# Seven products for pairs of output tiles in the q, k, v projections of a two-layer backbone step

## The chip, the cores and the metric

The kernel runs on one core of a Trainium2 chip. The metric is the device time of one execution in microseconds (us). The text calls the engines by their profile names: PE is TensorE's matmuls and PEld its weight loads, DVE is VectorE, ACT is ScalarE, POOL is GpSimd, SP is SyncE, which here only issues DMAs.

## The reference

The step runs a trunk of two layers over 1152 tokens of width 1024: 128 prompt tokens and 1024 latent tokens. Layer 0 mixes tokens by a gated long convolution, layer 1 by differential attention over 8 heads with rotary positions for the latent tokens. Each layer is followed by a feed-forward with a depthwise convolution of width 3. Every part has a norm ahead of it and one behind it, with shift, scale and gate from a small matrix product of the condition (the modulation). Cut to what the change touches:

```python
hp = modulate(rmsnorm(xp, norm_w[i, 0]), mp[0], mp[1])
hs = modulate(rmsnorm(xs, norm_w[i, 0]), ms[0], ms[1])
qp, kp, vp = qkv_heads(hp, at_w_qkv[j])           # h @ w_qkv: 1024 -> 3 * 1024
qs, ks_, vs = qkv_heads(hs, at_w_qkv[j])
qs = rope_2d(qs, cos_s, sin_s)                    # x * cos + rot * sin
ks_ = rope_2d(ks_, cos_s, sin_s)
ys = diff_attention(qs, k_all, v_all, ...)        # scores scaled by 64 ** -0.5 = 0.125

def conv_ffn(h, w_up, w_dw, b_dw, w_down):
    u = dwconv3(h @ w_up, w_dw, b_dw)
    g, val = jnp.split(u, 2, axis=-1)
    return (jax.nn.silu(g) * val) @ w_down
```

## The kernel before

The 1152 tokens are nine tiles of 128, T0 (the prompt) to T8, in three chunks of three tiles. The code counts the chunks 0, 1 and 2; the change's title calls them 1, 2 and 3. Activations lie with the model's width on the partitions (8 pieces of 128, index `k`) and tokens in the free dimension. To keep float32 precision every operand is split into `hi` (rounded) and `lo` (the rest), and each product is made as hi·hi + hi·lo + lo·hi, three matmuls. `split` (L214) does it: ScalarE writes `hi` (L215), then VectorE subtracts (L220); with `dma=True` ScalarE also writes `-hi` (L217) and GpSimd issues a DMA that adds the source to it (L218).

The stages follow each other: layer 0's mixer, its feed-forward, the projections to q, k, v, the attention, layer 1's feed-forward. What each engine does stands in the order in which the code was recorded; each engine takes its own row of instructions strictly one after the other and waits on the others by semaphores. So the order of the calls in the Python code decides what can hide behind what. Side work is written as generators: `advance(queue, n)` takes `n` steps of the queued ones, `advance(queue, -1)` runs the queue out, and `next(extra)` takes one row of the modulation's weights (a 512 KB load `adaw` and two DVE passes, L379).

*Feed-forward.* Chunk 0 goes group by group (up, convolution, down). Chunks 1 and 2 of the up projection go together by seven products: the weights of an output pair are a 2x2 block matrix (output tile by half of the inner dimension), the two chunks' activations another, and seven products of blocks with sums of blocks take the place of eight. `combine` makes the seven operands of the activations (`pair`, with `t` for the differences, ACT L553 and DVE L547, L560); the table `ALONG` says in which of the seven slots of a step the loads, the sums of the weights (`total`), their splits (`high`, `low`, `both`) and the evacuations of the banks are issued, and how many steps ahead. Slots from -19 on run along the last groups of chunk 0 (`along2`). The down projection of chunk 1 and then of chunk 2 follows (`down`), three or two weight tiles a group.

*Projections* (`groups`). 24 output tiles of 128, in the order q0 k0 v0 q1 k1 v1 ... (`ORDER`). For each tile and chunk a group of 24 matmuls (L1646 to L1648: 8 pieces by 3 products) of 386 or 384 columns; the first three tiles go chunk by chunk, the next 18 tile by tile, the last three together. ACT takes a group out of its bank, for chunk 0 in two pieces (L1652 the prompt, L1653 two latent tiles), else in one (L1655), and scales q by 0.125. The split of tile i+1 (`split_w`) is issued right behind the first of tile i's three groups. While the first groups run, the pre-norms of T6 to T8 are finished (POOL L457 `xn`, PE transposes L470, ACT L473, DVE L480 and L481). When a tile's three groups are there, `finish` turns q and k by position: eight DMAs of POOL (L1565) swap rows into `rot`, three DVE operations (L951) multiply and add, the result is split and stored. PE also does the prompt's own attention there, head by head (`Context`).

## Time and profile before

| what | time |
|---|---|
| median of 3 runs | 3126.3 us (3124.62 to 3126.78) |
| the profiled execution | 3126.71 us |
| its span from first to last instruction | 3124.9 us |
| projections within it, 1524.9 to 1855.3 | 330.4 us |
| down groups of the first feed-forward, chunk 1, 1333 to 1425 | 92 us |

The profiled execution's own time is 1.8 us more than its span, which lies around the instructions. The trace names source lines with L; matmuls are pipelined, so that the durations of two neighbours overlap, and the distance of their starts is what one costs. Behind "<-" in brackets stands what ended a wait, and ahead of it how long the engine had been idle.

### The profile page before, as it was taken

The numbers are of one execution on the slowest core, as the hardware profiler recorded it, in microseconds if no ns is written. First come the engines' busy times: TensorE is split into PE (matmuls) and PEld (weight loads), VectorE is DVE, ScalarE is ACT, GpSimd is POOL, SyncE is SP. The second block draws the span as 40 slices with busy tenths as digits, with TensorE's granted clock in tenths as the row PEclk, the third lists the DMA queues.
The fourth block names the chain that finished last, engine by engine and source line by source line (L and its number), as shares of the span: only waits on it lengthen the run. The fifth ranks groups of instructions, "written<-read, shape, count | busy, mean of one in ns | idle before, by whom it ended". The sixth has DMA issues, their size and how long they took to land. (4 is left out here: it accounts for less than half of the span.)

```text
span 3124.9 us, 46695 instructions
## 1 busy us (share of the span) xinstructions
PE 3044.9 (97%) x17332; PEld 2823.7 (90%) x17332; DVE 2143.6 (69%) x3057; ACT 1729.7 (55%) x3185; POOL 619.2 (20%) x1010
## 2 busy tenths in 40 slices
PE   8999999999998999999999999999999999999998
PEld 5999999778888999988899999999888998999987
DVE  5778888756676787776563347789565756777743
ACT  5454445545544777655533348899545546777532
POOL 3111111220001222211143422223220002222100
PEclk9999999999999999999999999999999999999999
DMA  6455546754445898777464464353363246887763
GB/s 254 114 125 119 125 114 157 212 187 141 149 156 154 211 214 209 168 290 258 149 196 148 134 194 110 96 145 106 135 212 140 96 161 153 215 183 182 218 212 119
DMA packets 190136, 520.48 MB, mean 167 GB/s; under 512 B 25730, under 2 KB 53986, under 8 KB 189908
## 3 DMA queue, kind: packets, MB, share of 16 engines
q1 hardware_dynamic: 137428, 394.94, 37.9%
q0 software_dynamic: 52480, 122.56, 19.5%
q8 instruction: 136, 2.23, 0.3%
q14 instruction: 92, 0.75, 0.1%
HBM read 354.50 MB, written 68.13 MB: 135 GB/s over the span
## 5 line engine op out<-in xcount | busy, mean ns | idle before, releaser
L746 PE MATMUL banks<-pair,hi 128*128 128x386 f32 x2464 | 639.1, 341 | 10.0 <-DVE junk L599 9.8
L746 PEld LDWEIGHTS banks<-pair,hi 128*128 128x128 f32 x2464 | 453.2, 190 | 11.4 <-DVE junk L599 10.7
L215 ACT ACTIVATE hi<-wr 128x1024 fp32r<-128x1024 f32 (+1 forms) x400 | 365.2, 913 | 150.4 <-DMA wr<-ffn_up 47.6
L220 DVE TENSOR_TENSOR lo<-wr,hi 128x1024 fp32r<-128x1024 f32 x247 | 305.4, 1237 | 204.8 <-ACT hi L215 203.4
L746 PE MATMUL banks<-pair,lo 128*128 128x386 f32 x1232 | 419.1, 340 | 0.7 <-DMA lo<-wr 0.7
L218 POOL DMA_DIRECT2D lo<-wr x153 | 132.5, 866 | 860.9 <-ACT lo L217 637.4
L690 PE MATMUL banks<-lo,hi 128*128 128x512 f32 x792 | 250.2, 396 | 5.9 <-DVE lo L220 5.9
L690 PE MATMUL banks<-hi,hi 128*128 128x512 f32 x792 | 251.7, 398 | 2.3 <-ACT hi L215 2.3
L690 PE MATMUL banks<-hi,lo 128*128 128x512 f32 x792 | 249.9, 395 | 0.0
L667 PE MATMUL banks<-hi,hi 128*128 128x388 f32 x704 | 240.6, 342 | 8.5 <-ACT hc L510 8.2
L669 PE MATMUL banks<-hi,lo 128*128 128x388 f32 x704 | 239.1, 340 | 1.8 <-DVE lo L220 1.8
L668 PE MATMUL banks<-lo,hi 128*128 128x388 f32 x704 | 239.7, 340 | 0.0
L746 PEld LDWEIGHTS banks<-pair,lo 128*128 128x128 f32 x1232 | 233.3, 189 | 1.0 <-DMA lo<-wr 1.0
L1746 DVE TENSOR_REDUCE mx<-banks 128x1 f32<-128x1152 f32 x128 | 173.4, 1356 | 68.9 <-PE banks L1741 61.7
L1340 PE MATMUL banks<-hi,hi 128*128 128x386 f32 (+1 forms) x576 | 200.4, 348 | 3.8 <-DVE hi L2072 2.5
L1342 PE MATMUL banks<-hi,lo 128*128 128x386 f32 (+1 forms) x576 | 197.1, 342 | 5.8 <-DMA lo<-wr 5.7
L1646 PE MATMUL banks<-hi,hi 128*128 128x384 f32 (+1 forms) x576 | 198.9, 345 | 0.0
L217 ACT ACTIVATE lo<-hi 128x512 fp32r<-128x512 f32 (+1 forms) x265 | 187.0, 706 | 18.6 <-DMA lo<-wr 6.2
L1648 PE MATMUL banks<-hi,lo 128*128 128x384 f32 (+1 forms) x576 | 196.0, 340 | 0.5 <-DVE lo L220 0.5
L1341 PE MATMUL banks<-lo,hi 128*128 128x386 f32 (+1 forms) x576 | 196.3, 341 | 0.0
L1647 PE MATMUL banks<-lo,hi 128*128 128x384 f32 (+1 forms) x576 | 195.9, 340 | 0.0
L690 PEld LDWEIGHTS banks<-lo,hi 128*128 128x128 f32 x792 | 148.8, 189 | 43.2 <-DVE lo L220 9.3
(386 smaller groups left out, 6869.5 us busy)
## 6 DMA issues: line engine op xcount, KB each, us to landing
wr<-ffn_up SPq DMA_DIRECT2D x176, 512.0 KB
wr<-ffn_down SPq DMA_DIRECT2D x132, 512.0 KB
lo<-wr POOLq DMA_DIRECT2D x132, 256.0 KB, 3.9
adaw<-w_adat SPq DMA_DIRECT2D x56, 512.0 KB
lo<-s POOLq DMA_DIRECT2D x88, 256.0 KB, 3.9
x<-x_d SPq DMA_DIRECT2D x33, 512.0 KB
hid<-cv SPq DMA_DIRECT2D x44, 384.0 KB
hd<-hid SPq DMA_DIRECT2D x88, 192.0 KB
```

The lines of the kernel that those rows point to most:

```text
L215: act.activation(hi, src, AF.Copy)
L220: dve.tensor_tensor(out=lo, in0=src, in1=f(hi), op=ALU.subtract)
L667: pe.matmul(pt[:, 0:n], wh[:, k, :], hh[:, k, 0:n], start=k == 0, stop=False)
L668: pe.matmul(pt[:, 0:n], wh[:, k, :], hl[:, k, 0:n], start=False, stop=False)
L669: pe.matmul(pt[:, 0:n], wl[:, k, :], hh[:, k, 0:n], start=False, stop=k == KT - 1)
L690: pe.matmul(accs[c][i][h], s_[:, o:o + P], w_[:, 512 * h:512 * h + 512], start=first and n == 0, stop=last and n == len(parts) - 1)
L746: pe.matmul(pt[:, 0:NP], w[:, k, :], t[:, k, :], start=q < 4 and k == 0 and i == 0, stop=k == 3 and i == 2, skip_group_check=q > 3)
L1340: pe.matmul(pt[:, 0:n], wh[:, k, :], hh[:, k, 0:n], start=k == 0, stop=False)
L1341: pe.matmul(pt[:, 0:n], wh[:, k, :], hl[:, k, 0:n], start=False, stop=False)
L1342: pe.matmul(pt[:, 0:n], wl[:, k, :], hh[:, k, 0:n], start=False, stop=k == KT - 1)
L1646: pe.matmul(pt[:, 0:m], wh[:, k, :], hh[:, k, b:b + m], start=k == 0, stop=False)
L1648: pe.matmul(pt[:, 0:m], wl[:, k, :], hh[:, k, b:b + m], start=False, stop=k == KT - 1)
```

## The change

Chunks 1 and 2 of the projections now go by seven products too, two output tiles at a time: 12 steps of 7 products of 12 matmuls of 384 columns. The code of the products becomes a class, `Seven`, that the feed-forwards share.

- Layer 1's pre-norm hands its output to `combine` as in the feed-forward, without the two halo columns (`n=384`); for T3 to T8 its own hi and lo on DVE fall away.
- The first eight tiles' chunk-0 groups run first (`EARLY`), with weights loaded and split for them alone; behind each of them come `split_w(i + 1)`, up to three steps of the queue, in which `combine` stands too, and in the last ones four slots of the table. Then the queue is run out, and the steps begin.
- From step 4 on, a step's operands are kept and used for the chunk-0 groups of its two tiles as well, behind products 4 and 6; the last of these comes inside the attention. Chunk 0 goes into `x0` first (L1689, L1690) and is copied into `xs` when the pair is finished (L1695).
- The factor 0.125 for the latent q moves into the rotation.
- The table `ALONG` is shorter: weights are loaded at slot 0 two steps ahead (slot 2, three steps ahead before), the sums 1 and 2 and the split of 1 are made one step ahead instead of two, and the first slot is -14. What only the feed-forward does in the slots is in `FILL`.
- The down groups of chunk 1 take two modulation rows each instead of one.

```diff
-    def prenorm_pair(T, x, ab, hs):
+    def prenorm_pair(T, x, ab, hs, n=NP):
...
+        e = (n - 3 * P) // 2
         if T in (2, 5):
-            hs["h", c + 1] = bt([KT, NP], "hc")
+            hs["h", c + 1] = bt([KT, n], "hc")
...
-            dst = h[:, :, 1 + P * i:1 + P * i + P]
+            dst = h[:, :, e + P * i:e + P * i + P]
...
-        if T == 2:
+        if e and T == 2:
...
-    def combine(hs):
+    def combine(hs, n=NP):
...
-            pair[q] = [mem([P, 4, NP], F32R, nm("pair")) for _ in range(2)]
+            pair[q] = [mem([P, 4, n], F32R, nm("pair")) for _ in range(2)]
...
+    class Seven:
...
+        TAKE = ((0, 0), (4, 1), (5, 2), (3, 3), (1, 0), (6, 2), (2, 3))
+        ALONG = (
+            ((2, "load"), (0, "total", 4), (0, "spare"), (-1, "evac", 6)),
+            ((1, "both", 0), (0, "high", 6), (0, "evac", 0)),
+            ((1, "total", 1), (0, "low", 6), (0, "evac", 1)),
+            ((1, "both", 2), (1, "total", 2), (0, "evac", 2)),
+            ((1, "high", 1), (1, "both", 3), (0, "evac", 3)),
+            ((1, "low", 1), (1, "both", 5), (0, "evac", 4)),
+            ((1, "both", 4), (2, "total", 3), (0, "evac", 5)))
+        FIRST = -14
+
+        def __init__(self, steps, n, fetch, hs, block, whole=()):
+            self.steps, self.n, self.fetch, self.hs, self.block, self.whole = steps, n, fetch, hs, block, whole
+            self.raw, self.ops, self.sums, self.out = {}, {}, {}, {}
+
+        def along(self, t):
+            j, q = divmod(t, 7)
+            for d, fn, *args in self.ALONG[q]:
+                if 0 <= j + d < self.steps:
+                    getattr(self, fn)(*args, j + d)
+
+        def load(self, j):
+            self.raw[j] = self.fetch(j)
...
+        def high(self, q, j):
+            self.ops[j, q] = bt([4, P], "hi", F32R), bt([4, P], "lo", F32R)
+            act.activation(self.ops[j, q][0], self.weight(q, j), AF.Copy)
+
+        def low(self, q, j):
+            hi, lo = self.ops[j, q]
+            dve.tensor_tensor(out=lo, in0=self.weight(q, j), in1=f(hi), op=ALU.subtract)
+
+        def both(self, q, j):
+            self.ops[j, q] = halves(self.weight(q, j), bt, [4, P], True)
+
+        def spare(self, j):
+
+            if j in self.whole:
+                self.ops[j, 7] = halves(self.raw[j][1][:, 0:4], bt, [4, P], True)
+
+        def product(self, j, q):
+            b, d = self.TAKE[q]
+            if q < 4:
+                self.out[j, d] = ps("pp", True)
+            pt = self.out[j, d]
+            wh, wl = self.ops[j, q] if j in self.whole else self.ops.pop((j, q))
+            bh, bl = self.hs["pair"][b]
+            for k in range(4):
+                for i, (w, t) in enumerate(((wh, bh), (wh, bl), (wl, bh))):
+                    pe.matmul(pt[:, 0:self.n], w[:, k, :], t[:, k, :], start=q < 4 and k == 0 and i == 0,
+                              stop=k == 3 and i == 2, skip_group_check=q > 3)
...
+        seven = Seven(NJ, NP, load_two, hs, block)
...
-        ALONG = (
-            ((-1, middle, 1), (0, total, 4), (-2, finish), (-1, evac, 6)),
-            ((-1, side, 1, 0), (-1, side, 1, 1), (1, both, 0), (0, high, 6), (0, evac, 0)),
-            ((3, load_pair), (-1, middle, 0), (2, total, 1), (0, low, 6), (0, evac, 1)),
-            ((1, both, 2), (-1, side, 0, 0), (2, total, 2), (0, evac, 2)),
-            ((2, high, 1), (1, both, 3), (-1, side, 0, 1), (0, evac, 3)),
-            ((2, low, 1), (1, both, 5), (0, evac, 4)),
-            ((-1, silu), (1, both, 4), (2, total, 3), (0, evac, 5)))
+        FILL = (((-1, middle, 1), (-2, finish)), ((-1, side, 1, 0), (-1, side, 1, 1)), ((-1, middle, 0),), ((-1, side, 0, 0),),
+                ((-1, side, 0, 1),), (), ((-1, silu),))
...
-                if t >= -19:
+                if t >= Seven.FIRST:
...
-                product(j, q)
+                seven.product(j, q)
...
                     next(extra, None)
+                    if c == 1:
+                        next(extra, None)
...
-                tt(xs, xs, rope[0], MUL)
-                tt(rot, rot, rope[1], MUL)
+                z = 0.125 if p == 0 else 1.0
+                for x, r in ((xs, rope[0]), (rot, rope[1])):
+                    dve.scalar_tensor_tensor(out=x, in0=x, scalar=z, in1=r, op0=MUL, op1=MUL)
...
+        EARLY = 8
+        out, heads_of = {}, {}
...
+        seven = Seven(len(ORDER) // 2, 3 * P, load_two, hs, block, range(EARLY // 2, len(ORDER) // 2))
+
+        def first_chunk(i):
+            if i < EARLY:
+                wh, wl = spl.pop(i)
+                ws = [(wh[:, k], wl[:, k]) for k in range(KT)]
+            else:
+                ops = [seven.ops.pop((i // 2, q)) for q in ((0, 4), (7, 5))[i % 2]]
+                ws = [(wh[:, k], wl[:, k]) for wh, wl in ops for k in range(4)]
+            hh, hl = hs[0]
+            pt = ps("pr")
+            for k in range(KT):
+                wh, wl = ws[k]
+                pe.matmul(pt[:, 0:386], wh, hh[:, k, 0:386], start=k == 0, stop=False)
+                pe.matmul(pt[:, 0:386], wh, hl[:, k, 0:386], start=False, stop=False)
+                pe.matmul(pt[:, 0:386], wl, hh[:, k, 0:386], start=False, stop=k == KT - 1)
+            x = heads_of[i] = st([3 * P], "x0")
+
+            act.activation(x[:, 0:P], pt[:, 1:1 + P], AF.Copy, scale=0.125 if ORDER[i][0] == 0 else 1.0)
+            act.activation(x[:, P:3 * P], pt[:, 130:386], AF.Copy)
+
+        def whole(i):
+
+            xs, x = out.pop(i), heads_of.pop(i)
+            act.activation(xs[:, 0:256], x[:, P:3 * P], AF.Copy)
+            return xs, x[:, 0:P]
...
-            runs = [range(3)] + [range(i, i + 1) for i in range(3, last - 3)] + [range(last - 3, last)]
-            seq = [(i, c) for r in runs for c in range(3) for i in r]
+            steps = last // 2
...
+            queue.append(combine(hs, 3 * P))
...
-                if i < 3:
-                    if n == 1:
-                        split_w(3)
-                    if n == 4:
-                        load_w(4)
-                elif i < last - 3:
-                    if c == 0:
-                        split_w(i + 1)
-                        load_w(i + 2)
-                    if i == last - 4 and c > 0:
-                        split_w(i + 1 + c)
-                        load_w(i + 2 + c)
...
+            for i in range(EARLY):
+                first_chunk(i)
+                if i + 1 < EARLY and i > 1:
+                    split_w(i + 1)
+                if i + 2 < EARLY and i > 0:
+                    load_w(i + 2)
+                advance(queue, 3 if i else 0)
+                if i == 3:
+                    load_rope()
+                if i > 3:
+                    next(const, None)
+                for t in range(4 * (i - EARLY), 4 * (i - EARLY) + 4):
+                    if t >= Seven.FIRST:
+                        seven.along(t)
+            advance(queue, -1)
+            for t in range(7 * steps + 1):
+                k, q = divmod(t, 7)
+                if k < steps:
+                    seven.product(k, q)
+                seven.along(t)
+                pend = [g for g in pend if next(g, g) is not g]
+                if q == 0 and k:
+                    for i in (2 * k - 2, 2 * k - 1):
+                        if i < last - 1:
+                            pend.append(finish(i, whole(i)))
+                            next(pend[-1])
+                if k in seven.whole and (q == 4 or q == 6 and k < steps - 1):
+                    first_chunk(2 * k + (q == 6))
+                if q in (2, 5):
                     next(extra, None)
...
+                if k > steps - 3 and q == 6:
+                    next(first, None)
+            yield
+            first_chunk(last - 1)
+            pend.append(finish(last - 1, whole(last - 1)))
...
-        yield from prenorm(T, x, ab_a[0], hs1, False)
+        yield from prenorm_pair(T, x, ab_a[0], hs1, 3 * P)
```

ScalarE in the projections, where one tile follows the other. Before, a tile in the middle (`xp` and `xs` are its chunk 0, then the next tile's `hi`):

```order
L1652 ACTIVATE xp_17158<-banks 128x128
L1653 ACTIVATE xs_17156<-banks 128x256
L215 ACTIVATE hi_17187<-wr_17052 128x1024
L1512 ACTIVATE ctx_17064<-banks 128x128
L215 ACTIVATE qh_17197<-xs_16887 128x1024
L1607 ACTIVATE v_17205<-banks 128x512
L1655 ACTIVATE xs_17156<-banks 128x384
L1607 ACTIVATE v_17205<-banks 128x512
L1655 ACTIVATE xs_17156<-banks 128x384
L1611 ACTIVATE ctx_17064<-banks 128x128
L1652 ACTIVATE xp_17283<-banks 128x128
L1653 ACTIVATE xs_17281<-banks 128x256
```

And now, from the fourth early group to the sixth (`x` is the new `x0`):

```order
L1689 ACTIVATE x_16142<-banks 128x128
L1690 ACTIVATE x_16142<-banks 128x256
L215 ACTIVATE hi_16147<-wr_16091 128x1024
L555 ACTIVATE pair_16155<-hc_14575 128x1536
L1689 ACTIVATE x_16188<-banks 128x128
L1690 ACTIVATE x_16188<-banks 128x256
L215 ACTIVATE hi_16193<-wr_16151 128x1024
L555 ACTIVATE pair_16202<-hc_14575 128x1536
L1689 ACTIVATE x_16240<-banks 128x128
L1690 ACTIVATE x_16240<-banks 128x256
L215 ACTIVATE hi_16245<-wr_16198 128x1024
```

`hi` of the next tile has moved from ahead of two more groups of its tile to the place between one group's evacuation and the next group. VectorE's `lo` follows each `hi`.

VectorE where the first tiles are done. Before, the split of the fifth tile, then the rotations of q0 and k0 begin:

```order
L220 TENSOR_TENSOR ckl_16315<-ck_16312,ckh_16314 128x128
L220 TENSOR_TENSOR lo_16356<-wr_16134,hi_16354 128x1024
L379 SCALAR_TENSOR_TENSOR adaj_16364,mcol_98<-adaw_15747,cb_14722 128x1024
L379 SCALAR_TENSOR_TENSOR adaw_15747,mcol_98<-adaw_15747,cb_14724 128x1024
L951 TENSOR_TENSOR xs_15922<-xs_15922,rope_16103 128x1024
L951 TENSOR_TENSOR rot_16207<-rot_16207,rope_16105 128x1024
L951 TENSOR_TENSOR xs_15922<-xs_15922,rot_16207 128x1024
L220 TENSOR_TENSOR ql_16403<-xs_15922,qh_16401 128x1024
L951 TENSOR_TENSOR xs_15954<-xs_15954,rope_16103 128x1024
L951 TENSOR_TENSOR rot_16245<-rot_16245,rope_16105 128x1024
```

And now, from the split of the sum for product 1 on, when the last early group is in (`pair_16385` is the `lo` of operand 4, `pair_16411` that of operand 5):

```order
L677 TENSOR_TENSOR s_16359<-s_16315,wr_16211 128x512
L691 TENSOR_TENSOR lo_16362<-s_16359,hi_16361 128x512
L677 TENSOR_TENSOR s_16380<-wr_16306,wr_16307 128x512
L562 TENSOR_TENSOR pair_16298<-t_16254,pair_16297 128x1536
L549 TENSOR_TENSOR t_16390<-hc_14575,t_16347 128x1536
L562 TENSOR_TENSOR pair_16385<-t_16347,pair_16384 128x1536
L549 TENSOR_TENSOR t_16399<-hc_15705 128x1536
L562 TENSOR_TENSOR pair_16394<-t_16390,pair_16393 128x1536
L562 TENSOR_TENSOR pair_16404<-hc_15705,pair_16402 128x1536
L562 TENSOR_TENSOR pair_16411<-t_16399,pair_16409 128x1536
```

On ScalarE these pieces' other halves stand behind the last early group's evacuation (`x_16342`) and the splits for step 0:

```order
L1689 ACTIVATE x_16342<-banks 128x128
L1690 ACTIVATE x_16342<-banks 128x256
L215 ACTIVATE hi_16354<-s_16303 128x512
L217 ACTIVATE lo_16355<-hi_16354 128x512
L687 ACTIVATE hi_16361<-s_16359 128x512
L215 ACTIVATE hi_16364<-s_16315 128x512
L217 ACTIVATE lo_16365<-hi_16364 128x512
L215 ACTIVATE hi_16370<-wr_16212 128x512
L217 ACTIVATE lo_16371<-hi_16370 128x512
L215 ACTIVATE hi_16375<-wr_16211 128x512
L217 ACTIVATE lo_16376<-hi_16375 128x512
L555 ACTIVATE pair_16384<-t_16347 128x1536
```

The rotations now come in the first steps, behind the operands of the pairs.

VectorE in the down groups of chunk 1, first feed-forward (`lo` of a hidden tile and of its weights in turn; `adaj` and `adaw` are the two passes of a modulation row). Before:

```order
L220 TENSOR_TENSOR lo_15115<-hd_14974,hi_15114 128x384
L220 TENSOR_TENSOR lo_15122<-wr_14972,hi_15120 128x1024
L220 TENSOR_TENSOR lo_15127<-hd_14981,hi_15126 128x384
L220 TENSOR_TENSOR lo_15134<-wr_14979,hi_15132 128x1024
L379 SCALAR_TENSOR_TENSOR adaj_15171,mcol_98<-adaw_15072,cb_14722 128x1024
L379 SCALAR_TENSOR_TENSOR adaw_15072,mcol_98<-adaw_15072,cb_14724 128x1024
L220 TENSOR_TENSOR lo_15213<-hd_15055,hi_15211 128x384
L220 TENSOR_TENSOR lo_15220<-wr_15053,hi_15218 128x1024
```

And now:

```order
L379 SCALAR_TENSOR_TENSOR adaj_14494,mcol_98<-adaw_14401,cb_14391 128x1024
L379 SCALAR_TENSOR_TENSOR adaw_14401,mcol_98<-adaw_14401,cb_14393 128x1024
L379 SCALAR_TENSOR_TENSOR adaj_14499,mcol_98<-adaw_14492,cb_14391 128x1024
L379 SCALAR_TENSOR_TENSOR adaw_14492,mcol_98<-adaw_14492,cb_14393 128x1024
L220 TENSOR_TENSOR lo_14540<-hd_14367,hi_14539 128x384
L220 TENSOR_TENSOR lo_14546<-wr_14365,hi_14545 128x1024
L220 TENSOR_TENSOR lo_14551<-hd_14374,hi_14550 128x384
L220 TENSOR_TENSOR lo_14557<-wr_14372,hi_14556 128x1024
L379 SCALAR_TENSOR_TENSOR adaj_14591,mcol_98<-adaw_14497,cb_14391 128x1024
L379 SCALAR_TENSOR_TENSOR adaw_14497,mcol_98<-adaw_14497,cb_14393 128x1024
```

Two rows stand between two groups' splits, where one stood.

## Rows read from the trace of the kernel before

**Rows 1.** Page, part 1: busy time, share and instructions of each engine.

```profile
PE 3044.9 (97%) x17332; PEld 2823.7 (90%) x17332; DVE 2143.6 (69%) x3057; ACT 1729.7 (55%) x3185; POOL 619.2 (20%) x1010
```

**Rows 2.** Stretches: from:to, length, busy us (x count) per engine, granted clock, DMA share, GB/s.

```profile
1524.90:1855.30 330.40, 326.79 (x1883) 321.66 (x1882) 146.61 (x189) 112.14 (x274) 120.43 (x238) 1.00 0.55 167
1333.00:1425.00 92.00, 91.38 (x406) 73.39 (x405) 71.02 (x97) 48.93 (x85) 12.13 (x12) 1.00 0.78 282
```

**Rows 3.** Waits of PE in the projections, 1524.9 to 1855.3: us, times, longest.

```profile
PE banks L470 <- POOL xn L457: 1.8, 2, 1.4
PE banks L1511 <- DVE ctx L1536: 1.3, 1, 1.3
PE banks L1648 <- DVE lo L220: 0.5, 1, 0.5
```

**Rows 4.** Timeline of PE inside one group: start, duration, line, operation.

```profile
1699.77 0.34 PE L1647 MATMUL banks<-lo,hi 128*128 128x384 f32 x1
...
1702.08 0.34 PE L1648 MATMUL banks<-hi,lo 128*128 128x384 f32 x1
```

**Rows 5.** Timeline of POOL and PE at the last pre-norm tile.

```profile
1536.85 1.13 POOL L457 TENSOR_SCALAR xn<-x,r 128x1024 f32<-128x1024 f32 x1
...
1536.38 0.43 PE L1646 MATMUL banks<-hi,hi 128*128 128x386 f32 x1
```

**Rows 6.** Timeline of PE, ACT, DVE where one tile follows the other.

```profile
1711.14 0.34 PE L1648 MATMUL banks<-hi,lo 128*128 128x386 f32 x1
...
1711.52 0.28 ACT L1652 ACTIVATE xp<-banks 128x128 f32<-128x128 f32 x1 [3.69 <-PE banks L1648]
...
1711.95 1.06 ACT L215 ACTIVATE hi<-wr 128x1024 fp32r<-128x1024 f32 x1
...
1609.34 1.22 DVE L220 TENSOR_TENSOR lo<-wr,hi 128x1024 fp32r<-128x1024 f32 x1
...
1610.61 0.44 PE L1648 MATMUL banks<-hi,lo 128*128 128x386 f32 x1 [0.51 <-DVE lo L220]
```

**Rows 7.** Groups by shape: line, engine, names, shapes, count, busy us, mean ns, idle before.

```profile
L220 DVE TENSOR_TENSOR lo<-wr,hi 128x1024 fp32r<-128x1024 f32 x22 | 26.9, 1224 | 112.6 <-ACT hi L215 112.6
L215 ACT ACTIVATE hi<-wr 128x1024 fp32r<-128x1024 f32 x22 | 23.3, 1060 | 3.4 <-DMA wr<-at_qkv 3.4
L379 DVE SCALAR_TENSOR_TENSOR adaw<-adaw,cb 128x1024 f32<-128x1024 f32 x8 | 9.8, 1225 | 0.3
...
L217 ACT ACTIVATE lo<-hi 128x512 fp32r<-128x512 f32 x101 | 64.0, 633 | 6.7 <-PE banks L746 3.6
L732 DVE TENSOR_TENSOR lo<-s,hi 128x512 fp32r<-128x512 f32 x39 | 26.7, 684 | 1.7 <-ACT hi L729 1.6
...
L553 ACT ACTIVATE pair<-t 128x1544 fp32r<-128x1544 f32 x4 | 6.0, 1496 | 7.0 <-DVE t L547 7.0
...
L560 DVE TENSOR_TENSOR pair<-t,pair 128x1544 fp32r<-128x1544 f32 x4 | 7.0, 1758 | 0.0
L547 DVE TENSOR_TENSOR t<-hc,t 128x1544 f32<-128x1544 f32 x2 | 3.5, 1759 | 0.0
```

**Rows 8.** Timeline of PE after idle stretches, and the granted clock there.

```profile
50.79 0.44 PE L1340 MATMUL banks<-hi,hi 128*128 128x388 f32 x1 [1.73 <-DVE hi L2072]
...
1008.03 1.01 PE L746 MATMUL banks<-pair,hi 128*128 128x386 f32 x2 [4.46 <-DVE junk L599]
1008.83 0.53 PE L746 MATMUL banks<-pair,lo 128*128 128x386 f32 x1
...
1011.73 0.52 PE L746 MATMUL banks<-pair,lo 128*128 128x386 f32 x1
...
2609.84 1.01 PE L746 MATMUL banks<-pair,hi 128*128 128x386 f32 x2 [5.38 <-DVE junk L599]
...
2608.00:2616.00 8.00, 6.17 (x26) 6.17 (x27) 6.81 (x12) 4.03 (x12) 3.53 (x7) 0.66 0.45 97
```

**Rows 9.** Timeline of ACT before the second feed-forward's products.

```profile
2605.26 0.63 ACT L217 ACTIVATE lo<-hi 128x512 fp32r<-128x512 f32 x1 [2.64 <-DMA lo<-wr]
```

More of the change, by code (lines that the diff above doesn't have):

```diff
@@ L737, in product @@
-        def product(j, q):
-            b, d = SEVEN[q]
-            if q < 4:
-                out[j, d] = ps("pp", True)
-            pt = out[j, d]
-            wh, wl = ops.pop((j, q))
-            bh, bl = hs["pair"][b]
-            for k in range(4):
-                for i, (w, t) in enumerate(((wh, bh), (wh, bl), (wl, bh))):
-                    pe.matmul(pt[:, 0:NP], w[:, k, :], t[:, k, :], start=q < 4 and k == 0 and i == 0,
-                              stop=k == 3 and i == 2, skip_group_check=q > 3)
```

168 lines of the change are left out of this document (64 added, 104 removed).

## The prediction

> **What bounds the kernel now.** The page's first part comes first [rows 1]: TensorE has matmuls in flight for 97% of the span, the next engine, VectorE, for 69%. A share over the whole span doesn't say what the changed stretch is worth, so the table by stretches is next [rows 2]. The projections to q, k and v run from 1524.9 to 1855.3 us: 330.4 us, PE busy for 326.8 of them, VectorE for 146.6, ScalarE for 112.1, at full clock. The waits of PE in that stretch add up to 3.6 us [rows 3]. So the stage is as long as its matmuls, and every other engine has more than half of its time to spare. Inside a group one matmul starts 0.178 us after the other (13 steps in 2.31 us) [rows 4]; the 0.34 us that each row shows overlap. 24 tiles x 3 chunks x 8 pieces of the inner dimension x 3 products are 1728 matmuls, 307.6 us of the 330.4; transposes, the prompt's scores and the 3.6 us of waits are the rest. Fewer matmuls help here only as far as the other engines keep handing over operands in time, and that is where I looked longest.
>
> **The change part by part.** All times are made against the profiled run, 3126.7 us, which is 0.4 above the median of the runs, 3126.3.
>
> Matmuls. Chunk 0 keeps 24 x 24 = 576. Chunks 1 and 2 took 24 x 2 x 24 = 1152; now 12 pairs x 7 products x 12 = 1008. That is 144 less at 0.178 us: **-25.6 us**. Nothing else on PE goes away.
>
> Pre-norm of the last three latent tiles. Before, PE met the last tile's transposes after group 2 and so had work meanwhile: it went on with group 2 at 1536.38, while GpSimd's last `xn` ended at 1537.98 [rows 5]. Now three steps of the queue are taken after each early group, and all three tiles' first transposes stand ahead of group 2. It starts 0.5 us (four transposes) after 1537.98, at 1538.5 instead of 1536.4: **+2.1**. Bounds: 0, if GpSimd came earlier by that much, and 3.
>
> The eight early groups. In the order of the program, ScalarE first takes group i from its bank and only then makes `hi` of tile i+1; VectorE's `lo` follows, and PE's group i+1 needs both at once. Before, the same `hi` stood right behind the first of the tile's three groups, so that two groups, 8.5 us, hid it. Now nothing hides it. From the start of a group's last matmul to the evacuation are 0.38 us, to the start of `hi` 0.81 us (1711.14, 1711.52, 1711.95) [rows 6]; `hi` takes 1.06, `lo` 1.22 [rows 7], and PE follows 0.05 behind `lo` (1610.56, 1610.61) [rows 6]. The third matmul of the next group is the first that needs `lo`: it starts 3.14 us after that last matmul, where 0.53 (three steps) would do. That is 2.6 us for each of groups 4 to 7, and about 1.6 for group 3, ahead of which some 1 us of transposes runs: **+12.0**. ScalarE's extra row, a piece of the pairs, lies between `hi` and the next evacuation, in 4 us without work, so I count it at nothing; without that cover it is 1.5 a group.
>
> From the last early group to the products. After group 7 (let it end at E) the queue is run out, so four of the seven operand sums are still to come, and on ScalarE they stand behind nine pieces of 512 columns for the weights of step 0. Those start at E+0.6 and take 9 x 0.63 = 5.7 [rows 7]. The `hi` of pair 4, 1.50 us, ends at E+7.8, its `lo` on VectorE, 1.76, at E+9.6. Pair 5 has its `lo` at the end of VectorE's row: one subtraction and three `lo`, 4 x 1.76 = 7.0, so E+16.6. Product 1 waits for pair 4, product 2 for pair 5. Product 2 then has eleven matmuls left and ends at E+18.6, where 3 x 2.14 = 6.4 would do: **+12.2**. Bounds: 7, if the nine pieces found room earlier, and 14. Products 3 to 6 use pairs that are ready, so nothing of it is given back.
>
> The clock after a wait. Where PE had stood for 4.46 or 5.38 us, the granted clock of the stretch is low (0.66 of full in 8 us) and matmuls start 0.322 us apart, nine steps from 1008.83 to 1011.73, 1.2 GHz instead of 2.4 [rows 8]. After 1.73 us without a matmul they kept the full pace [rows 8]. In the passage to the products PE stands for 5.4 us ahead of product 1 (its slow matmuls end before pair 5 is there) and for about 4 us inside product 2: eleven matmuls x 0.144 = **+1.6**; bounds 0 and 4.
>
> Steps 1 to 3 have no chunk-0 group between their products, 84 x 0.178 = 15.0 us each. In step 1 VectorE has to do the rotation of two heads and their `lo`, 8 x 1.22 = 9.8, and four sums, two `lo` and five additions, 11 x 0.68 = 7.5 at most [rows 7]: 17.3 us. It comes 2.3 late, and steps 2 and 3, with one head each, inherit some: **+4**, bounds 0 and 8. From step 4 on, two chunk-0 groups make a step 23.5 us, and VectorE catches up. The extra 256-column copies on ScalarE (112 us busy of 330 [rows 2]), twice the weight loads for the first eight tiles and the 0.125 moved into the rotation are hidden.
>
> The first feed-forward. Eight rows of the modulation weights move from the projections into the down groups of chunk 1. Each is two passes of 1.225 us [rows 7], 19.6 us together. VectorE is busy there for 71.0 of 92.0 us, the DMA engines for 0.78 [rows 2]; 90.6 of 92.0 remains possible. I take **+1**, between 0 (it all fits) and 5.6 (below).
>
> The shorter table in both feed-forwards changes no matmul, and the pieces ahead of the first evacuation stand in the same number on ScalarE. The two stalls at the start of the products, 4.46 and 5.38 us [rows 8], may shrink or grow: **0**, between -12.7 and +4.
>
> Sum: -25.6 + 2.1 + 12.0 + 12.2 + 1.6 + 4 + 1 + 0 = +7.3. Against the median that is 3126.3 + 7.3 = **3133.6 us**.
>
> **The rivals.** *The gain arrives.* If the splits came early enough, what is left is -25.6 + 2.1 + 1 = -22.5: 3103.8. With half of the two passages (6.0 and 6.1) and 2 for the rotation, it is -8.4: 3117.9. For it: ScalarE and VectorE are idle for more than half of the stage [rows 2]. Against it: the order, in which `hi` stands behind the evacuation that ends the group before. This is also the case in which the count alone decides.
>
> *Not slower, by the feed-forwards.* One place, the start of the products, twice: there ScalarE waits 2.64 us for a DMA ahead of the second one, before it turns to the evacuations [rows 9]. If the shorter table lets that wait go and with it both stalls, 4.46 + 5.38, and ten slow matmuls after each, 2 x 1.44, the gain is 12.7: 3120.9, within 0.2%. It decides from 1.0 us on. Against it: the same pieces stand there on ScalarE.
>
> *The clock falls in the early groups too.* Five groups, each with a gap of some 1.6 us and another of 0.8. If eleven matmuls run slowly after each, that costs 5 x 1.6 = 8.0: 3141.6. Against it stands the row at 50.79, where 1.73 us left the pace as it was [rows 8]. The Trainium skill (TensorE: Matmul & The Clock Gate, "HAM oscillation — how this bites in real kernels") says that a loop of short bursts and waits for data pays for the return to half rate in every turn. [...]
>
> *Chunk 1's down groups run out of VectorE.* 21.0 us idle less 19.6 leave 1.4. If a third of that idle time, 7.0, can't be used because VectorE waits there for ScalarE, the groups come 5.6 late, 4.6 above my term: 3138.2, more if the added loads come late too.
>
> **How the numbers follow.** A difference below 0.2%, 6.3 us, can't be told from none, so "same" is 3120.0 to 3132.6. The forecast has 0.45, with its own range 3126 to 3141: 0.26 slower, 0.19 same. The gain 0.14, faster. The feed-forwards 0.13: 0.09 same, 0.04 faster. The clock 0.16, slower. The down groups 0.12: 0.11 slower, 0.01 same. Together faster 0.18, same 0.29, slower 0.53. The range 3110 to 3146 leaves out most of the full gain (0.1) and what adds up on the slow side (0.1).
>
> **What would show it.** Right: waits of PE for `hi` and `lo` in groups 3 to 7, some 7 us from one to the next; a wait of about 5 and one of about 4 us for the pairs behind group 7; the stage at about 337 us; a low clock behind group 7 alone. Wrong: groups 4.3 us apart, a first step below 20 us, or a stage below 320 us; a low clock at 1545 to 1575 would be the third rival, waits in 1333 to 1425 the fourth, and shorter stalls ahead of the products the second.

## The result, and the profile after

The changed kernel takes 3237.7 us (3234.4 to 3241.6), the one before 3126.5: 1.0357 times as long, interval 1.0339 to 1.0375, 111 us slower. The forecast was 3133.6, the range up to 3146. The profiled execution took 3241.6 us, its span is 3239.7.

The page's first part and the clock's slices, which answer to [rows 1]. PE has a little more busy time although 144 of its instructions are gone (17188 for 17332), and there are two slices in which the clock isn't full:

```profile
PE 3062.5 (95%) x17188; PEld 2829.5 (87%) x17188; DVE 2206.2 (68%) x3170; ACT 1813.0 (56%) x3336; POOL 682.9 (21%) x1078
...
PEclk9999999999999999999889999999999999999999
```

The stretches come next, as in [rows 2] (from:to, length, busy us and count of PE, PEld, DVE, ACT and POOL, granted clock, DMA share, GB/s). The first is the down groups of chunk 1, the second the whole of the projections, and the last three are its parts: the early groups, the passage to the products, the steps.

```profile
1333.00:1440.00 107.00, 98.82 (x437) 79.26 (x436) 86.07 (x124) 54.35 (x89) 14.39 (x10) 0.98 0.76 278
1542.60:1965.40 422.80, 332.61 (x1713) 318.42 (x1712) 193.48 (x272) 197.47 (x426) 180.45 (x308) 0.89 0.64 166
1543.00:1606.00 63.00, 47.97 (x220) 43.69 (x220) 21.85 (x26) 31.73 (x65) 9.26 (x13) 0.86 0.36 124
1606.00:1627.00 21.00, 14.63 (x53) 13.14 (x53) 17.38 (x17) 14.96 (x21) 5.29 (x7) 0.67 0.61 128
1627.00:1965.40 338.40, 269.61 (x1441) 261.24 (x1440) 154.25 (x231) 150.78 (x341) 165.90 (x289) 0.90 0.70 176
```

The projections take 422.8 us; [rows 2] had 330.4 for the stretch, which ran some microseconds into the attention (324.6 from its first matmul to the attention's first score). PE is busy for 332.6 of the 422.8, DVE for 193.5, ACT for 197.5: none of them is the bound. The granted clock is 0.89. The work up to the attention is 65 x 24 = 1560 matmuls (the last of the 1584 come inside the attention), 1560 x 0.178 = 278 us, and some 18 of the rest, as much as before (324.6 less 1704 x 0.178 and 3.6 of waits). PE is idle for 422.8 - 332.6 = 90 us, and of its busy time some 37 are more than that work needs at full clock. The waits of PE in that stretch, which answer to [rows 3]:

```profile
PE banks L1607 <- DMA kc<-cache_k: 43.8, 7, 12.2
PE banks L710 <- DVE xs L733: 18.9, 8, 5.3
PE banks L1684 <- ACT hi L215: 6.6, 5, 1.6
...
PE banks L1686 <- DVE lo L220: 3.2, 5, 0.7
PE banks L508 <- POOL xn L457: 3.2, 3, 1.4
...
PE banks L710 <- DVE v L721: 1.8, 1, 1.8
```

The stages, from the first matmul of each to the first of the next (the attention's from its first score to its last), in us, of this kernel and of those of the experiments below. Each column is one profiled execution, up to some 4 us from the median of its kernel; the stages left out differ by at most 3 us from before:

| stage | before | after | b_lag | b_table | b_table94 | a_split | a_pairs | a_pairsall |
|---|---|---|---|---|---|---|---|---|
| up to the first feed-forward | 689.6 | 697.5 | 697.1 | 683.1 | 686.2 | 697.1 | 678.8 | 686.1 |
| its chunk 0 | 300.4 | 300.2 | 302.6 | 286.8 | 297.7 | 300.1 | 286.8 | 297.6 |
| its seven products | 343.5 | 343.5 | 344.9 | 338.5 | 343.9 | 343.7 | 338.4 | 344.5 |
| its down groups | 191.2 | 201.4 | 190.8 | 190.1 | 191.3 | 201.4 | 200.5 | 201.3 |
| projections | 324.6 | 422.8 | 325.2 | 324.6 | 325.8 | 403.9 | 371.7 | 332.5 |
| attention | 350.0 | 352.1 | 350.2 | 350.4 | 350.1 | 352.4 | 348.3 | 354.2 |
| second feed-forward's seven products | 338.3 | 335.6 | 338.1 | 335.1 | 335.4 | 335.6 | 334.0 | 333.5 |

So 98 of the 115 us of span are lost in the projections, 10 in the down groups, and 8 ahead of the first feed-forward, where the change touches no instruction. Inside the projections, the first matmuls of the 12 steps lie 28.8, 28.6, 24.0, 25.9, 38.1, 27.8, 33.0, 31.8, 26.4, 30.7, 31.1 and 35.9 us apart; the products and chunk-0 groups alone would need 15.0 in steps 0 to 3, 23.5 in steps 4 to 10 and 19.2 in step 11, which has one such group.

What PE waits for most is a load of 64 KB: the cached keys `kc` of a head, which are transposed (L1607) with the prompt's keys. The view of that tile, before and then after (line, engine, operation, count, duration min/median/max in ns, first and last start):

```profile
L1568 SPq DMA_DIRECT2D kc<-cache_k x8: 327/328/432, 1541.2 to 1801.9; - x8
...
L1576 PE MATMUL banks<-ident,kc x8: 272/273/273, 1568.8 to 1818.8; 128*128 128x128 f32 x8
```

```profile
L1599 SPq DMA_DIRECT2D kc<-cache_k x8: 327/328/877, 1636.5 to 1940.3; - x8
...
L1607 PE MATMUL banks<-ident,kc x8: 273/476/477, 1641.7 to 1946.5; 128*128 128x128 f32 x8
...
  PE banks L1607: 43.8, 7
```

Before, the first load was issued at 1541.2 and used at 1568.8; now it is issued at 1636.5 and used at 1641.7. Over the eight heads it was 14 to 31 us from issue to use; now it is 2.6 to 9.1.

All buffers lie in one arena of on-chip memory. A plan made ahead of time gives each its place, and whoever fills a buffer waits until the last user of that place is through. A piece of the chain that ended last shows one head, with the row of PE that it ends in (start, us, what; then PE's row with its idle time):

```profile
1713.89 8.33 DMA lo<-wr
...
1722.34 2.42 DMA kc<-cache_k
...
1724.97 0.48 PE L1607 MATMUL banks<-ident,kc 128*128 128x128 f32 x1 [9.50 <-DMA kc<-cache_k]
```

The load of the keys waits some 8 us until a DMA that makes the `lo` of a weight has landed. It reads an input of the kernel, so it can only be waiting for its place; in the plan it takes the place of that weight, which that DMA reads. Then it needs 2.4 us, and PE, in whose row the transpose stands ahead of the next product, has stood for 9.5. SP's own waits for its loads of weights and keys in the stage are of that kind (SP's queue, line, what it waited for: us in total, times, longest): the weight loads (L1662) wait for stores of earlier heads, and the keys stand behind them.

```profile
SPq L1662 <- DMA kd<-qh: 53.4, 4, 21.6
SPq L1662 <- DMA qd<-qh: 41.1, 3, 25.5
...
SPq L1662 <- DMA lo<-wr: 37.0, 3, 29.7
...
SPq L1599 <- DMA lo<-wr: 20.1, 3, 8.6
```

The kernel before had such waits too; its key loads (L1568) waited 56 us in all, those of the changed kernel (L1599) 47. The two longest before:

```profile
SPq L1568 <- DMA new_k<-kt: 17.9, 2, 14.0
SPq L1568 <- DVE ql L220: 14.1, 1, 14.1
```

PE waited for none of them, because the loads were still issued well ahead of their use. So the waits for places alone weren't what cost time; they do where the lead over the use has become short.

### The profile page after: what moved, and what is told of

It is laid out like the page before. It is cut to its first block, busy times and chain, and to the rows that moved or that the text cites. A ratio compares the mean times of both kernels' runs of the same rounds, so it can differ in the third digit from the quotient of the medians.

```text
span 3239.7 us, 46924 instructions
## 1 busy us (share of the span) xinstructions
PE 3062.5 (95%) x17188; PEld 2829.5 (87%) x17188; DVE 2206.2 (68%) x3170; ACT 1813.0 (56%) x3336; POOL 682.9 (21%) x1078
## 5 line engine op out<-in xcount | busy, mean ns | idle before, releaser
L710 PE MATMUL banks<-pair,hi 128*128 128x386 f32 (+1 forms) x3136 | 830.9, 346 | 31.3 <-DVE xs L733 18.9
L710 PEld LDWEIGHTS banks<-pair,hi 128*128 128x128 f32 x3136 | 586.0, 194 | 36.7 <-DVE xs L733 21.1
L710 PE MATMUL banks<-pair,lo 128*128 128x386 f32 (+1 forms) x1568 | 540.3, 345 | 9.0 <-DVE lo L691 5.4
L220 DVE TENSOR_TENSOR lo<-wr,hi 128x1024 fp32r<-128x1024 f32 x231 | 284.3, 1231 | 130.8 <-ACT hi L215 122.3
L218 POOL DMA_DIRECT2D lo<-wr x197 | 171.8, 872 | 911.7 <-ACT lo L217 489.8
L710 PEld LDWEIGHTS banks<-pair,lo 128*128 128x128 f32 x1568 | 303.0, 193 | 10.3 <-DVE lo L691 6.0
L217 ACT ACTIVATE lo<-hi 128x512 fp32r<-128x512 f32 (+1 forms) x333 | 229.9, 690 | 28.9 <-DVE uA L982 6.1
L1795 PE MATMUL banks<-hd,hd 128*128 128x384 f32 x768 | 182.6, 360 | 3.0 <-DMA hd<-kd 1.8
L828 DVE SCALAR_TENSOR_TENSOR cv<-row,dw,cv 128x768 f32<-128x768 f32 x176 | 178.0, 1012 | 3.5 <-ACT cv L823 1.7
L785 PEld LDWEIGHTS banks<-hi,lo 128*128 128x128 f32 x792 | 150.1, 190 | 34.4
```

The source lines that it names most:

```text
L217: act.activation(lo, f(hi), AF.Copy, scale=-1.0)
L218: pool.dma_start(lo, src, accum_op=ALU.add)
L220: dve.tensor_tensor(out=lo, in0=src, in1=f(hi), op=ALU.subtract)
L710: pe.matmul(pt[:, 0:self.n], w[:, k, :], t[:, k, :], start=q < 4 and k == 0 and i == 0, stop=k == 3 and i == 2, skip_group_check=q > 3)
L785: pe.matmul(accs[c][i][h], s_[:, o:o + P], w_[:, 512 * h:512 * h + 512], start=first and n == 0, stop=last and n == len(parts) - 1)
L1795: pe.matmul(sbank[m][:, b, 0:SP], Q[:, m, q0:q0 + P], K[:, m, b * SP:b * SP + SP], start=i == 0, stop=i == 1)
```

## The experiments

**The plan's distance.** Two suspicions had to be told apart for the 8 us ahead of the change. The plan keeps a place free for 40 program steps after a DMA has used it, or for a part of them where not all fit. With the changed kernel's buffers it found only 20, and this run gives the kernel before the same 20.

```diff
-    for part in (4, 3, 2, 1, 0):
+    for part in (2, 1, 0):
```

> The kernel before, with one number changed: the plan that lays the buffers into the arena keeps a buffer that a DMA reads or writes free for 20 program steps after its last use, as the changed kernel's plan does, instead of 40. Nothing else moves. Theory A (the shorter distance costs time everywhere): about +10 us up to the end of the first feed-forward's chunk 0, in the same places as in the changed kernel (long convolution +5, output projection +3, chunk 0 +2), 3135 to 3145 in all. Rival (those +10 come from the changed kernel's own plan, other neighbours in memory, not from the distance): within 3 us of the kernel before.

Measured: 3141.9 us, 1.0053 of before (1.0037 to 1.0070). The stages up to the first feed-forward take 697.1 us, those of the changed kernel 697.5. A plan with the shorter distance makes these 8 us without any instruction of the change. In the whole kernel it costs 16 us; the old order's projections lose next to nothing by it (325.2 for 324.6).

**The modulation rows.**

```diff
                     next(extra, None)
+                    if c == 1:
+                        next(extra, None)
```

> The kernel before, with two modulation rows a group in the down groups of chunk 1 instead of one, as in the changed kernel; the projections keep none of them. Theory (VectorE and the loads run out there): the down groups take about 10 us more, as in the changed kernel (201 instead of 191 us), some of it given back in the projections: 3130 to 3137. Rival (the +10 of the changed kernel there comes from its buffers): within 2 us of the kernel before.

Measured: 3132.8 us, 1.0022 (1.0013 to 1.0032), 7.4 us slower. In the profiled execution, which is 3.1 us above that median, the down groups take 203.4 us, with PE waiting for DVE's `lo` there (waits; then the stretch of chunk 1):

```profile
PE banks L690 <- DVE lo L220: 7.5, 5, 3.7
```

```profile
1331.40:1440.00 108.60, 99.97 (x424) 78.62 (x424) 88.06 (x128) 51.69 (x91) 19.58 (x14) 0.97 0.76 275
```

DVE is busy for 88.1 of 108.6 us and still late: the two rows, four passes of 1.22 us, stand in a block ahead of the `lo` that the next group needs. And in that block DVE itself stood idle, 5.4 and 4.1 us, for the load of a second row (before, its waits for such loads came to 1.6 us here):

```profile
DVE adaj L379 <- DMA adaw<-w_adat: 9.5, 2, 5.4
```

PE's two longest waits, 3.75 and 1.87 of the 7.5 us, come right behind these two. So passes and loads are both in it, and no run parts them. Some of it comes back in the projections (322.4 us).

**The table alone.** The class with its shorter table in the feed-forwards, and nothing else of the change.

```diff
-            ((3, load_pair), (-1, middle, 0), (2, total, 1), (0, low, 6), (0, evac, 1)),
+            ((2, "load"), (0, "total", 4), (0, "spare"), (-1, "evac", 6)),
...
-                if t >= -19:
+                if t >= Seven.FIRST:
```

> The kernel before, with the new class and its shorter table in the two feed-forwards alone; projections, pre-norm and modulation rows as before. Theory (the table is a small gain, as the second feed-forward of the changed kernel shows, 4 us shorter): 3118 to 3124. Rival (no effect): within 2 us.

Measured: 3098.8 us, 0.9914 of before (0.9900 to 0.9929), 27 us faster and the fastest kernel of this study. That is far more than expected, and most of it lies where the table has hardly anything to do: 6.5 us ahead of the first feed-forward, and 13.6 in its chunk 0, which takes 286.8 us for 300.4. The stretch of chunk 0 before, with b_table, and with the next kernel:

```profile
689.60:990.00 300.40, 286.24 (x1477) 264.36 (x1477) 208.39 (x277) 141.66 (x212) 7.82 (x11) 0.98 0.45 155
```

```profile
683.10:969.90 286.80, 281.77 (x1477) 262.19 (x1477) 206.77 (x274) 142.03 (x214) 8.15 (x11) 1.00 0.47 162
```

```profile
686.20:983.80 297.60, 285.45 (x1477) 264.36 (x1477) 206.79 (x274) 142.61 (x214) 8.15 (x11) 0.99 0.44 153
```

The shorter table holds fewer weights at a time, so the plan may fill the arena to 98% as it spreads the buffers, where it had found 94% before. The next run takes that away again:

```diff
-        for percent in range(100, 70, -2):
+        for percent in range(94, 70, -2):
```

> b_table (the kernel before with the shorter table in the feed-forwards) with one number changed: the plan of the buffers may fill the arena to 94% only when it spreads them, as the kernel before's plan had to, instead of 98%. No instruction moves. Theory A (most of b_table's gain is room: the shorter table holds fewer weights, so the plan can keep places idle longer, in stages that the table doesn't touch too): the time up to the feed-forward is back at 687 to 691 us and its chunk 0 at 297 to 301, 12 to 20 us slower than b_table, 3110 to 3120. Rival (the gain is the table's own order): within 4 us of b_table, 3095 to 3103.

Measured: 3119.3 us, 0.9982 of before (0.9973 to 0.9992). 20 of the 27 us are the plan's. The 5 that are left need not be the table's own: by the stages 6 us are gained ahead of the products of the first feed-forward and 3 in the second's, some are lost elsewhere, and this plan too has other places than the one before.

**The keys.**

```diff
+            if ORDER[i][0] == 1:
+                keys[ORDER[i][1]] = st([P], "kc")
+                sync.dma_start(keys[ORDER[i][1]], a["cache_k"][ORDER[i][1]])
             hh, hl = hs[0]
...
-                    kc = st([P], "kc")
-                    sync.dma_start(kc, a["cache_k"][j])
+                    kc = keys.pop(j)
```

> The changed kernel, with the load of a head's cached keys issued with the chunk-0 group of its k tile instead of in finish, two products ahead of the transposes that need it. Theory A (in SyncE's row the load stands behind weight loads that wait for buffers, and TensorE waits for it in every head): the waits at the transposes, 44 us, go, and with them the slow matmuls behind each: 3165 to 3185. Rival B (the steps of finish come twice as fast as before, and every hand-over in it is late): TensorE waits at the next one, for the rotated rows and the banks, and the gain is 10 to 25 us: 3212 to 3227.

Measured: 3230.3 us, 1.0336 of before (1.0315 to 1.0357), some 7 below the changed kernel; less than the 10 of the rival. The projections fall by 14.4 us to 408.4, and the attention takes 5.4 more. The 44 us of waits for the keys are gone, and PE now waits for the evacuations (first two rows, PE), since DVE waits in turn (last two): for the place of `v`, which a store of the keys had read last, and for the rotated rows.

```profile
PE banks L710 <- DVE xs L733: 26.2, 7, 6.2
PE banks L710 <- DVE v L721: 25.7, 5, 7.2
...
DVE v L721 <- DMA kcd<-ckh: 16.2, 2, 8.6
DVE xs L1619 <- DMA rot<-xs: 15.3, 5, 4.5
```

So the order in SP's row is worth 14 us of the stage at most; with the keys in time, the next hand-over holds PE.

**Room.** From step 1 on the products that take operands 4 to 6 (products 1, 2 and 5; the expectation below names them by their operands) read operands 0 to 2 again, and 36 KB of each partition come free. The instructions are the same, and the kernel leaves out what these operands carry, so its projections have other values.

```diff
             b, d = self.TAKE[q]
+            if self.whole and j:
+                b %= 4
```

> The changed kernel with room in the arena: from step 1 on products 4, 5 and 6 read the operands 0, 1 and 2 of the activations again instead of their own, so that 36 KB of each partition come free there (of 206); every instruction stays, and the plan of the buffers finds its full distance of 40 steps for the whole program. The projections' values differ for that. Theory M (with 192 to 203 KB taken all through the stage, each new buffer waits for the engine or DMA that used its place last, and the engines hold each other up): the stage falls from 423 to 335 to 350 us, the time up to the feed-forward by 10 to 25: 3115 to 3150. Rival P (the steps of finish come twice as often as before, one product instead of one group apart, so rotated rows and cached keys come late whatever the room): the stage stays above 390 us, 3195 to 3215.

Measured: 3151.6 us, 1.0083 of before (1.0054 to 1.0112), 86 us below the changed kernel. The projections fall by 51 us to 371.7, at a clock of 0.94; the stages ahead of them are 38 us shorter than in the changed kernel; b_table's were 26 shorter than before. The stretch of the projections and what is left of PE's waits there:

```profile
1504.60:1876.30 371.70, 312.85 (x1713) 299.84 (x1712) 191.26 (x272) 195.51 (x426) 185.47 (x308) 0.94 0.73 189
```

```profile
PE banks L1609 <- DMA kc<-cache_k: 18.4, 3, 13.4
PE banks L712 <- DVE xs L735: 15.9, 6, 5.2
```

Room is the largest cause, but not the whole one: the expectation was 335 to 350. With that room the plan also finds its full 40 steps of distance where it had 20, so this run doesn't tell free memory from distance.

> As a_pairs, and the cached keys loaded with the chunk-0 group of their tile, as in a_kc. If SyncE's row holds the keys up even with room in the arena, this is 10 to 40 us below a_pairs; if the room was the cause of that too, within 5 us of it.

The edits are those of a_pairs and a_kc together. Measured: 3166.5 us in all, 15 more than a_pairs, since the plan came out at 94% and the stages ahead of the projections take 26 us more; the projections themselves take 363.3 us, 8 less than in a_pairs.

> As a_pairs, and the steps of finish at every second product, so that they are 4.3 us apart or more, as before. Theory P's share: what is left of TensorE's waits for the rotated rows and the keys goes, 10 to 40 us below a_pairs. Rival (room alone): within 5 us of a_pairs.

```diff
-                pend = [g for g in pend if next(g, g) is not g]
+                if t % 2:
+                    pend = [g for g in pend if next(g, g) is not g]
```

Measured: 3167.1 us, again by another plan; the projections take 359.9 us, 12 less. In the whole, both expectations missed, because the plan moves other stages by more than the edit moves its own. Their projections can be compared with those of a_pairs, but only roughly, since the plan differs there too: they give each hand-over some 10 us.

**The early splits.**

```diff
             for i in range(EARLY):
-                first_chunk(i)
                 if i + 1 < EARLY and i > 1:
                     split_w(i + 1)
                 if i + 2 < EARLY and i > 0:
                     load_w(i + 2)
+                first_chunk(i)
```

> The changed kernel with the split of the next early tile issued ahead of the chunk-0 group, not behind it, for tiles 3 to 7. Theory (the order alone makes the waits of 1.6 and 0.7 us per group, and they put the matmuls behind them at the lower clock): groups 4.3 us apart instead of 7 to 9, full clock there, 15 to 20 us less in the early groups; of it 0 to 5 come back in the passage to the products, since the operands of the activations are not ready sooner: 3220 to 3228 all in all. Rival (weights are late too): under 5 us.

Measured: 3222.9 us, 1.0311 of before (1.0281 to 1.0341), 15 below the changed kernel. The last four early groups start at 1567.9, 1573.2, 1577.4 and 1581.6, at 0.96 of the clock over the stretch:

```profile
1543.00:1590.00 47.00, 39.41 (x217) 37.47 (x215) 22.70 (x28) 32.18 (x67) 9.42 (x13) 0.96 0.48 166
```

The stage is 18.9 us shorter, 17.0 of it in the early groups (43.3 for 60.3 from the first of them to the first product). The passage behind it takes 19.8 us from the first product to the fourth, as in the changed kernel (19.6).

**All together.** Room, keys, slower steps and early splits.

> The changed kernel with the room of a_pairs (its projections' values differ), the keys loaded with their tile's chunk-0 group, the steps of finish at every second product and the early splits ahead of their groups. Theory (room, late hand-overs and the order of the early splits together make up the stage's loss): the projections take 325 to 340 us, what is left above 301 being the passage to the products and a few waits: 3120 to 3140 in all, by the plan it finds. Rival (something else holds the stage): 350 us or more.

Measured: 3143.5 us, 1.0060 of before (1.0040 to 1.0080). The whole is just above the expected 3120 to 3140, with a plan at 94% again; the projections take 332.5 us, in the expected 325 to 340:

```profile
1529.50:1861.90 332.40, 306.67 (x1709) 297.44 (x1708) 188.36 (x270) 190.60 (x419) 178.78 (x302) 0.96 0.79 205
```

Steps 6 to 10 are 24.2 to 25.1 us apart, 0.7 to 1.6 more than their matmuls. What is left is the passage (29.2 us for step 0), two waits of 5.3 and 4.2 us, and the clock. Even with everything in time, and with room that the kernel doesn't have, the seven products come out 8 us behind the old order's 324.6.

**Fewer DMAs on the places.**

```diff
-            self.ops[j, q] = halves(self.weight(q, j), bt, [4, P], True)
+            self.ops[j, q] = halves(self.weight(q, j), bt, [4, P], not self.whole)
```

> The changed kernel with the early splits ahead of their groups, and in the projections the lo halves of the products' weights made by VectorE alone instead of ScalarE, a DMA and its adding. Nothing then waits for those DMAs when it takes a place in the arena over, and the plan finds a distance of 30 steps instead of 20. Theory (waits for DMAs on the arena's places are a large part of the stage's loss): the stage falls from 404 (a_split) to 360 to 380 us, 3180 to 3200 in all. Rival (VectorE, with 3.4 us more per step, becomes the bound in the steps of 15 us): within 10 us of a_split, 3213 to 3233.

Measured: 3195.1 us, 1.0225 of before (1.0204 to 1.0245), 28 below a_split; the projections take 376.8 us, as expected. DVE has 42 us more to do in the stage and it is 27 us shorter:

```profile
1542.80:1919.60 376.80, 314.73 (x1714) 303.06 (x1712) 234.69 (x340) 155.16 (x358) 120.04 (x240) 0.92 0.44 139
```

The edit takes the DMAs that make `lo` out of the steps, and with them SP's waits for `lo<-wr`, 57 us in the changed kernel. That fits a step that is held by transfers on its places, but it doesn't show which of them held which. SP's waits for other places grew instead (52 us for `rot<-xs`, 27 in a_split), PE's for the keys fell from 33.5 to 13.8 us, ACT and POOL have 41 and 61 us less to do, and the plan finds 30 steps of distance instead of 20. Those were not told apart.

## Why the prediction was wrong, point by point

The forecast called the kernel slower, and it is, but for the most part not for the reasons given. With its terms the projections would have taken 324.6 + 6.3 = 330.9 us; they took 422.8. Of the 92 us between, some 5 lie in the early groups and some 87 in steps 1 to 11. None of the rivals reached that far.

*Matmuls, -25.6.* Right: 144 instructions less, 0.178 us apart where PE doesn't wait and the clock is full. [rows 4]

*Pre-norm, +2.1.* Near: PE's waits there are 3.2 us, [rows 3] had 1.8.

*Early groups, +12.0.* Right in mechanism and near in size (11.1), and then the clock came on top. Timeline of PE (start, us, line, operation, count, idle before and what ended it):

```profile
1563.99 0.44 PE L1684 MATMUL banks<-hi,hi 128*128 128x386 f32 x1 [0.28 <-ACT hi L215]
...
1570.97 0.45 PE L1684 MATMUL banks<-hi,hi 128*128 128x386 f32 x1 [1.59 <-ACT hi L215]
1571.26 0.34 PE L1685 MATMUL banks<-lo,hi 128*128 128x386 f32 x1
1572.23 0.45 PE L1686 MATMUL banks<-hi,lo 128*128 128x386 f32 x1 [0.63 <-DVE lo L220]
...
1573.74 0.53 PE L1684 MATMUL banks<-hi,hi 128*128 128x386 f32 x1
1574.06 0.53 PE L1685 MATMUL banks<-lo,hi 128*128 128x386 f32 x1
...
1579.51 0.45 PE L1684 MATMUL banks<-hi,hi 128*128 128x386 f32 x1 [1.58 <-ACT hi L215]
```

Group 4 begins 6.98 us behind group 3; 4.27 + 2.6 = 6.9 was forecast. Its first matmul waits 1.59 us for `hi`, the third 0.63 for `lo`. But from 1573.74 on matmuls start 0.32 us apart, and the group takes 8.5 us. Groups 4, 5 and 6 take 8.5, 9.8 and 8.5 us, together 5.9 more than three at the 7.0 of group 3. This was the third rival, with a price of 8.0. a_split took 17.0 us out of the early groups: 5.9 of the clock and 11.1 of the waits, where 8.0 and 12.0 stood in the prediction. What misled here is the use of a single row [rows 8]: that one wait of 1.73 us left the pace as it was said nothing of waits of 1.6 and 0.6 that come back in every group. The loop that the Trainium skill describes (TensorE: Matmul & The Clock Gate, "HAM oscillation — how this bites in real kernels") is another one: its turn computes for less time than it then waits. Here a group's matmuls take 4.3 us and its two waits 2.2, and the clock over the early groups was 0.86, so the loss came without the page's condition.

*The passage, +12.2, and the clock behind it, +1.6.* Right in sum: from the first product to the fourth are 19.6 us, where 18.6 + 1.6 was forecast. That the sum is so close is in part luck, since it is made up otherwise. PE waits first for a weight's `lo`, which no term had, then for pairs 4 and 5:

```profile
1605.55 0.44 PE L710 MATMUL banks<-pair,lo 128*128 128x384 f32 x1 [1.96 <-DMA lo<-wr]
...
1610.50 0.45 PE L710 MATMUL banks<-pair,hi 128*128 128x384 f32 x1 [2.93 <-ACT pair L555]
...
1612.30 0.69 PE L710 MATMUL banks<-pair,hi 128*128 128x384 f32 x1 [1.35 <-DVE pair L562]
...
1617.15 0.69 PE L710 MATMUL banks<-pair,hi 128*128 128x384 f32 x1 [0.96 <-ACT pair L555]
...
1618.97 0.69 PE L710 MATMUL banks<-pair,hi 128*128 128x384 f32 x1 [1.14 <-DVE pair L562]
```

The waits for pairs 4 and 5 come to 4.3 and 2.1 us, where 5.4 and some 4 were forecast. The rest is slow matmuls, the granted clock being 0.67: they fill product 1 too, where the prediction charged eleven in product 2 alone.

*Steps 1 to 3, +4, and nothing from step 4 on.* **This is the step that failed.** Steps 1 to 11 take 333 us (1631.9 to 1965.2); their products and chunk-0 groups need 3 x 15.0 + 7 x 23.5 + 19.2 = 229, and the price put on the steps was 4 us. The working counted DVE's busy time against a step's length and found room. It counted no load and no store, though the change moves a step of `finish` from every group to every product, so that a load of the keys had 2.6 to 9.1 us instead of 14 to 31, and puts it right behind a step's two weight loads in SP's row. And it took the buffers as given. PE's waits in these steps come to 69 us. Of the 333 some 47 went with room in the arena and the longer distance that it allows (a_pairs: 286 us for these steps) and 27 more with the keys, the slower steps and the early splits (a_pairsall: 259). In a_pairsall 30 are left above the 229; they hold 13 us of waits, the transposes and the prompt's attention. Where the buffers stand close, the place of one is the queue of the other: engines wait for DMAs whose data they don't need.

*The first feed-forward's rows, +1, bounds 0 and 5.6.* Mis-sized, in the direction of the fourth rival: +10.2 in the down groups, +12.2 in b_ada's profiled execution, some 2 given back behind them, 7.4 in the whole kernel. DVE was idle for a fifth of the time; the busy share was no bound. The price was what stands ahead of the `lo`: four passes, and in two places a load that the second row waited for (9.2 us of DVE's time in the changed kernel). The rival had named late loads in passing; the term had none.

*The table, 0, between -12.7 and +4.* The second rival named the wrong place. PE's waits at the start of the products didn't shrink in all: 8.8 us in the first feed-forward and 2.6 in the second, for 5.2 and 5.4 before. But b_table shows a gain of 27 that the changed kernel doesn't get: with the projections' buffers the plan finds 20 steps and 94%, with b_table's 40 and 98%; a_pairs, which gets 40 and 98% as well, has b_table's times in the first feed-forward (286.8 and 338.4 us for 286.8 and 338.5).

*The buffers.* No term at all stood for the plan. It decides over 16 us of loss (b_lag) and 20 us of gain (b_table, b_table94), much of it in stages without an edit.

Left open: how the 47 us of the room divide between places of weights, keys and evacuated rows, and between free memory and the distance of 40 steps. None of them was given by itself.

## What to carry to other kernels

Where all buffers share one arena, a change that fills it in one stage has to be costed there for every load and store that may then wait for a place, and in every other stage for the distance that the plan loses; memory freed can be worth more than the instructions saved (86 us in a_pairs against 25.6). A generator that is stepped more often gives each load that it issues less time: for each, write down when it was issued and needed before, and when after the change. A busy share that fits says nothing when the order puts the long piece ahead of the one that is waited for.

## What the hardware showed

In the early groups PE waits 1.6 us and then 0.6 to 0.7 us once in every group of 24 matmuls. Behind these waits matmuls started 0.32 us apart for part of the group, the pace of the lower clock in [rows 8]. In the changed kernel that befell three groups in a row (8.5, 9.8 and 8.5 us); in a_pairs and a_kc, with the same instructions and waits there, only one (8.5 us, and 7.0 for the next two). Where the waits were gone (a_split), the clock was 0.96 over these groups for 0.86. A single wait of 1.73 us had cost nothing [rows 8]. What decides between one slow group and three, no run here shows.
